# Loads, stores and direct copies of a strided slice: turns by groups of eight batches, one batch per direct copy

## The chip, the cores and the metric

The kernel runs on one core of a Trainium2 chip. The time is device microseconds (us) of one execution; lower is better. Some executions come out slow: more than 1.5% above the fastest of the same kernel. They are left out, and kernels are compared by their fast executions alone, taken on the same chip in the same rounds. A run here is one kernel tried on the chip.

## The reference

```python
# x: float32 [32, 1024, 512]; start, stop, stride = 0, 512, 2
def reference(x, start, stop, stride):
    return x[:, start:stop:stride, :].astype(np.float32)      # [32, 256, 512]
```

Nothing is computed. Every second row of the first 512 rows of each batch is copied: 32 batches of 256 rows of 2 KB, 16.78 MB read and 16.78 MB written.

## The kernel before

Each batch is split by the parity of its output row. One half goes from DRAM to DRAM (a "direct copy", on the gpsimd queue). The other half goes through SBUF: a load and later a store. `apart(b)` says which half is which. A direct copy and a load each serve two batches (512 KB); a store serves one (256 KB).

```python
def apart(b):
    return 1 - (b >> 1 & 1)

def two(t, b, step, parity):       # rows of one parity, of the batches b and b + step
    return t[b : b + step + 1 : step].rearrange("b (p two) d -> two p b d", two=2)[parity]
...
for g in range(0, B, EIGHT):
    for i, (b, step) in enumerate(((0, 5), (2, 5), (1, 3), (3, 3))):
        b += g
        at = g + 2 * i
        (sp, act)[i % 2].dma_start(held[at // 2], two(src, at, 1, 1 - apart(at)))        # load
        pool.dma_start(two(out, b, step, apart(b)), two(src, b, step, apart(b)))         # direct
for b in range(B):
    to = out[b].rearrange("(p two) d -> two p d", two=2)[1 - apart(b)]
    sp.dma_start(to, held[b // 2][:, b % 2])                                             # store
```

All loads come before all stores in program order. The framework adds the waits: eight DMAs may be under way on the gpsimd queue, and eight on the sync and scalar queues together.

## Time and profile before

| what | value | how to read it |
|---|---|---|
| time | 79.45 us, median of 3 (79.29 to 79.64) | |
| span of the profiled execution | 77.4 us | first instruction to last |
| first and last data packet | 1.8 and 76.1 us | all DMA work lies between them |
| data packets' time / 16 engines | 73.0 us | 74.3 us lie between first and last packet, so engines are nearly never idle |
| direct copies ended | 55.6 us | of the gpsimd queue's packets |
| loads ended | 48.8 us | of the scalar queue's packets |

A 2 KB packet takes 84 ns in the median and a 4 KB packet of the gpsimd queue 159 ns. Throughout, **late** is a packet over 40 ns above that. **Excess** is all time above it, summed over packets; 16 us of excess cost 1 us of time, as there are 16 engines. **Idle** is the time from first to last data packet less all data packets' time / 16. The small packets that report a DMA's completion count as idle (0.6 us before), and packets that overlap make it smaller, so it is a net figure.

### The profile page before, as it was taken

To read this page: it belongs to the slowest core of one execution; us is meant where nothing else is said; L and a number is where in the kernel's file an instruction comes from. 1 tells how busy PE (TensorE), PEld (TensorE's weight loads), DVE (VectorE), ACT (ScalarE), POOL (GpSimd) and SP (SyncE) were. 2 spreads that over 40 slices of the span, in tenths; PEclk is the share of its full clock that TensorE was granted. 3 is DMA by queue.
4 is the path that set the end of the run, shared out by engine and by line. 5 is a ranking of instruction groups with operands and counts; after the bars stand their busy time and mean duration, and the time that the engine had idled before them with its cause. 6 is when DMAs were issued, how large, how long until landed. Compare 5 with 4: busy or idle time off the path is not lost. (4 is left out here: it accounts for less than half of the span.)

```text
span 77.4 us, 113 instructions
## 1 busy us (share of the span) xinstructions
POOL 11.3 (15%) x20
## 2 busy tenths in 40 slices
POOL 4995003303023031130000000000000000000000
DMA  0799999999999999999999999999999999999960
GB/s 7 235 303 334 332 281 347 327 310 386 351 349 363 364 314 358 358 321 333 323 300 310 347 307 357 413 392 339 402 404 405 375 356 347 361 356 353 350 216 20
DMA packets 11264, 25.17 MB, mean 325 GB/s; under 512 B 1024, under 2 KB 1024, under 8 KB 11264
## 3 DMA queue, kind: packets, MB, share of 16 engines
q1 hardware_dynamic: 6784, 12.59, 48.1%
q0 software_dynamic: 2304, 8.39, 29.3%
q10 hardware_dynamic: 2176, 4.19, 17.7%
HBM read 16.78 MB, written 16.78 MB: 434 GB/s over the span
## 5 line engine op out<-in xcount | busy, mean ns | idle before, releaser
L37 POOL DMA_DIRECT2D out_dram<-in_x_dram x16 | 11.1, 696 | 22.6 <-DMA out_dram<-in_x_dram 21.8
L57 POOL MEMSET const-float32-0.0<- 128x1 f32 x1 | 0.1, 99 | 0.2 <-issue 0.2
L57 POOL MEMSET const-bfloat16-1.0<- 128x1 bf16 x1 | 0.1, 102 | 0.0
L57 POOL MEMSET const-uint8-127<- 128x1 uint8 x1 | 0.1, 100 | 0.0
L57 POOL MEMSET const-float32-1.0<- 128x1 f32 x1 | 0.1, 99 | 0.0
## 6 DMA issues: line engine op xcount, KB each, us to landing
out_dram<-in_x_dram POOLq DMA_DIRECT2D x16, 512.0 KB, 23.6
out_dram<-held SPq DMA_DIRECT2D x32, 256.0 KB, 6.1
held<-in_x_dram ACTq DMA_DIRECT2D x8, 512.0 KB, 22.9
held<-in_x_dram SPq DMA_DIRECT2D x8, 512.0 KB, 22.7
```

Source lines behind the costliest of these rows:

```text
L37: pool.dma_start(two(out, b, step, apart(b)), two(src, b, step, apart(b)))
L57: nc = _bacc.Bacc("TRN2", target_bir_lowering=False, num_devices=1)
```

## The change

Its intent: reading and writing shall be mixed all along, instead of reading first and writing last. Loads run one group of eight batches ahead; then the group's stores follow on the same two queues. Direct copies are issued one batch at a time.

```diff
-    sp, act, pool = nc.sync, nc.scalar, nc.gpsimd
+    queues = (nc.sync, nc.scalar)
+    groups = range(0, B, EIGHT)
+
+    def one(t, b, parity):
+        return t[b].rearrange("(p two) d -> two p d", two=2)[parity]
+
     with tc.tile_pool(name="io", bufs=1) as io:
         held = [io.tile([P, 2, D], x.dtype, name=f"held{i}") for i in range(B // 2)]
-        for g in range(0, B, EIGHT):
-            for i, (b, step) in enumerate(((0, 5), (2, 5), (1, 3), (3, 3))):
-                b += g
-                at = g + 2 * i
-                (sp, act)[i % 2].dma_start(held[at // 2], two(src, at, 1, 1 - apart(at)))
-                pool.dma_start(two(out, b, step, apart(b)), two(src, b, step, apart(b)))
+
+        def load(g):
+            for b in range(g, g + EIGHT, 2):
+                queues[b // 2 % 2].dma_start(held[b // 2], two(src, b, 1, 1 - apart(b)))
+
+        def store(g):
+            for b in range(g, g + EIGHT):
+                queues[b % 2].dma_start(one(out, b, 1 - apart(b)), held[b // 2][:, b % 2])
+
         for b in range(B):
-            to = out[b].rearrange("(p two) d -> two p d", two=2)[1 - apart(b)]
-            sp.dma_start(to, held[b // 2][:, b % 2])
+            nc.gpsimd.dma_start(one(out, b, apart(b)), one(src, b, apart(b)))
+        load(0)
+        for g in groups:
+            if g + EIGHT < B:
+                load(g + EIGHT)
+            store(g)
```

Three things change: the turns, the second queue with stores, and one batch per direct copy.

## The prediction

> **What bounds the kernel now.** I read the page first for who works at all, then the queues, then stretches of the span, then the single packets.
>
> ```profile
> span 77.4 us, 113 instructions
> ...
> DMA  0799999999999999999999999999999999999960
> GB/s 7 235 303 334 332 281 347 327 310 386 351 349 363 364 314 358 358 321 333 323 300 310 347 307 357 413 392 339 402 404 405 375 356 347 361 356 353 350 216 20
> ...
> q1 hardware_dynamic: 6784, 12.59, 48.1%
> q0 software_dynamic: 2304, 8.39, 29.3%
> q10 hardware_dynamic: 2176, 4.19, 17.7%
> ```
>
> No compute engine matters. The 16 DMA engines are 90% busy or more in every slice but the first two and the last two, while the rate wanders between 281 and 413 GB/s. So nothing starves: the time is the sum of all packets' times over 16 engines. From the kernel, q0 is the gpsimd queue (direct copies), q10 the scalar queue (half of the loads), q1 the sync queue (the other half and all stores). The shares add to 95.1%, or 73.6 us of 77.4; the rest is the 1.8 us before the first data packet and the 1.3 us after the last (at 76.1).
>
> The chain of waits ends in direct copies, POOL line 37, only because it was followed along one queue; the issues show that the queues are deep:
>
> ```profile
> POOL out_dram L37 <- DMA out_dram<-in_x_dram: 21.8, 8, 4.8
> ...
> out_dram<-in_x_dram POOLq DMA_DIRECT2D x16, 512.0 KB, 23.6
> out_dram<-held SPq DMA_DIRECT2D x32, 256.0 KB, 6.1
> ```
>
> Eight direct copies waited, the last eight of 16: eight may be under way at once. The sync and scalar queues have eight places together (the fifth load of each waits for the first of its queue, and each store for the DMA eight before it). A direct copy lands 23.6 us after issue, so POOL's waits cost nothing.
>
> Stretches, chosen where the packets of a queue begin or end (us from the start; POOL, clock, DMA share, GB/s):
>
> ```profile
> 2.00:6.00 4.00, 4.00 (x7) 1.00 0.89 274
> 6.00:48.00 42.00, 6.36 (x10) 1.00 1.00 334
> 48.00:54.00 6.00, 0.00 (x0) 1.00 1.02 384
> 54.00:60.00 6.00, 0.00 (x0) 1.00 1.04 403
> 60.00:75.00 15.00, 0.00 (x0) 1.00 1.02 345
> ```
>
> 2 to 6 is loads alone, 6 to 48 loads and direct copies, 48 to 54 direct copies and stores, then stores alone. (The first store is issued at 30.9 but sits behind the loads of its queue.) The rate is 334 while loads run and 384 to 403 when they have ended: this is what the change aims at. Is the loss caused by running loads together, or does each load bring it along? For that I counted the packet records of the trace (duration and size of every packet). A 2 KB packet has a median of 84 ns, a 4 KB packet of q0 159 ns. "Late" is over 40 ns more; excess is what the packets took over 84 or 159 ns:
> - Loads, 6 to 48: 3567 packets, 334 late (9.4%), by 229 ns on average; excess 77.9 us. Loads alone, 2 to 6: 536, 51 late (9.5%); excess 11.6 us.
> - Direct copies beside loads, 6 to 48: 1646 packets, 137 late (8.3%), by 206 ns; excess 29.4 us. Beside stores, 48 to 54: 366, 25 late (6.8%), by 229 ns; excess 5.9 us.
> - Stores, 48 to 60: 1481 packets, none late, excess 0. After 60: 2575, mean 95 ns, excess 28.9 us, as a broad stretch (5% over about 124 ns) and not as single late packets.
>
> So a packet that reads DRAM is late in 7 to 9.5% of cases whatever stands beside it, and one that only writes is not. This is the core of my prediction: the cost goes with the packet, not with the order.
>
> **What the Trainium skill says.** "DMA: Bandwidth & Descriptors", section "Issuing engines are not separate DMA queues": all queues run on the same 16 engines, and several issuers save only sequencer time. The trace agrees: the share is already 1.00 with three queues and 1.04 with one. The same page, "Queues, rings and completion order": an engine takes turns between queues packet by packet. It agrees: from 6 to 48 q0 with 4 KB packets moved 6.74 MB, the two 2 KB queues 7.31 MB. The same page, "Where 436 GB/s comes from": a ceiling of 435 GB/s; the best stretch here is 403, and 2 KB in 84 ns on 16 engines is 390. "HBM Reference", section "Latency": an access takes 0.2 us on average and more under load; late packets are late by 206 to 229 ns, but no run yet shows why.
>
> **The change, part by part.**
> 1. Bytes, row size (2 KB) and the halves of the rows stay. Direct copies become 32 of 256 KB in place of 16 of 512 KB: 16 more DMAs, so 256 more completion packets of 9 ns, 2.3 us / 16 = 0.14 us. POOL needs 0.69 us an issue now; even at that, 32 take 22 us, beside 50 us of transfer. Eight in flight are now 2.1 MB, at half of 340 GB/s some 12 us of work: still deep. Cost 0.1 us.
> 2. Floor, unchanged: 8192 packets x 84 ns + 2048 x 159 ns = 1013.8 us.
> 3. Read excess, by the above unchanged: 11.6 + 77.9 + 29.4 + 5.9 = 124.8 us. Floor and read excess / 16 = 71.2 us.
> 4. Stores alone after 60 us cost 28.9 / 16 = 1.8 us extra. That is what mixing can win, since beside direct copies stores have none. How much is left? In round robin q0 gets half of the bytes, so direct copies again end near 54 us (8.39 MB at 175 GB/s is 48 us, from 6 on). By then the other two queues have moved some 9.5 MB: loads of two groups, stores of one, loads of the third and part of a store group. About 7.3 MB follow, of which the last two store groups, 4.2 MB, are stores alone: 2048 packets against some 3700 now. The stretched mode began about 6 us (1100 packets) into stores alone; so 900 packets x 11 ns / 16 = 0.6 us remain, and 1.2 us are won.
> 5. Waits. DMAs strictly alternate between sync and scalar, so the one eight before is on the same queue: four places each, 1 to 2 MB. Each store's load was issued at least 8 DMAs before it. A store group of four x 256 KB per queue is some 5 us of work against a landing spread of about 2 us: no gap, or a few tenths at turns. I allow 0.3 us.
>
> Sum: 71.2 + 0.6 (stretched stores) + 1.3 (ramp and completion packets: today's 74.3 us between first and last packet less 1167.5 / 16 = 73.0) + 0.1 + 0.3 = 73.5 us, plus 3.1 us at the ends = a span of 76.6. Time over span is 79.45 - 77.40 = 2.05 in medians, 79.17 - 77.40 = 1.8 in the profiled run. That gives 78.5; I take 78.3, since the 6.8% beside stores is a little under 9%.
>
> **The rivals.**
> - Reading is what is overcrowded. From 6 to 48 all that moves is being read (334 GB/s), from 48 to 54 only two thirds. If late reads come from crowding, a mix at 380 all along gives 25.17 MB / 380 = 66 us, and a time near 71 to 72. For it: the rise to 384 at 48 us, and 6.8 against 8.3%. Against it: 25 and 137 cases do not separate these, loads without direct copies are late as often, and the mean rises merely because stores replace loads.
> - Reads and writes disturb each other, or one batch per direct copy meets worse addresses (now each 4 KB packet pairs rows of two batches, then two rows of one). Late reads at 11% in place of 9 would add 125 x 2/9 / 16 = 1.7 us: 80 to 81. Stores beside direct copies show no disturbance, but loads beside stores stand nowhere in this trace.
> - Four places per queue run dry at each turn. Five turns at 0.7 us would bring 81 to 82. The landing spread of some 2 us against 5 us of work speaks against it.
> - The stretched stores come back whole, as they need only stores from two queues: 79.5.
>
> **Range and chances.** The middle, 78.3, stands 0.4 us over the 2% line (77.9), and gain rests on a mode I can't explain; crowding would be a far larger gain. So 75.6 to 80.8, with 0.36 for faster, 0.50 within, 0.14 slower.
>
> **What would show it.** Right: DMA share stays at 1.00, late reads at 8 to 9.5% in every stretch, excess of reads near 125 us in sum, stores at 84 ns beside direct copies, direct copies ended near 54 us, last stores somewhat stretched. Wrong: late reads clearly under 7% where stores run beside loads (crowding; far faster), over 10% (disturbance; slower), slices with a share under 0.95 at the turns (places run dry), or direct copies that end last.

## The result, and the profile after

The changed kernel takes 83.73 us (median of 4, 83.38 to 83.89), against 79.37 us for the kernel before in the same rounds. The ratio is 1.0547 (95% interval 1.0491 to 1.0604). Ratios throughout are the mean time of one kernel's fast runs over that of the other's in the same rounds, so not quite the ratio of the medians quoted. The prediction, 78.3 with a range up to 80.8, was wrong, and on the wrong side.

The page of the changed kernel, with the span, the rows by 40 slices of 2.05 us, and the queues (packets, MB, share):

```profile
span 82.1 us, 145 instructions
...
DMA  0999989999999999999999999999999999799920
GB/s 16 264 309 340 273 221 373 367 280 338 330 372 417 376 318 318 337 236 302 285 349 316 299 374 400 381 321 328 326 250 297 300 332 361 293 391 394 375 85 8
...
q1 hardware_dynamic: 4480, 8.39, 31.3%
q10 hardware_dynamic: 4480, 8.39, 31.0%
q0 software_dynamic: 2560, 8.39, 30.7%
```

The engines are nearly as busy as before, save for an 8 early on and a 7 near the end. The GB/s row has lost its shape: instead of a flat start and a fast later part it swings from 417 down to 236. The bytes are the same. Each byte of the gpsimd queue, q0, now takes longer: 30.7% of 82.1 us against 29.3% of 77.4.

Stretches of the changed kernel (from:to, length, POOL busy and count, clock, DMA share, GB/s):

```profile
22.00:28.00 6.00, 1.79 (x4) 1.00 1.03 385
34.00:38.00 4.00, 1.57 (x3) 1.00 1.00 267
48.00:52.00 4.00, 1.05 (x2) 1.00 1.04 395
58.00:64.00 6.00, 0.00 (x0) 1.00 0.99 283
70.00:74.00 4.00, 0.00 (x0) 1.00 0.92 349
```

```profile
28.00:34.00 6.00, 1.57 (x3) 1.00 1.06 333
52.00:58.00 6.00, 0.00 (x0) 1.00 1.06 337
69.00:71.00 2.00, 0.00 (x0) 1.00 0.73 280
```

By counting the packets of each queue in order one sees what stood at its head. From 23 and from 47 us on, both queues start a group of stores: 385 and 395 GB/s. From 34 and from 58 us on they turn from stores back to loads: 267 and 283 GB/s, with engines that are counted as busy. The stores before such a turn suffer first: loads are issued again at 28.8 and 53.0 us, and until the loads' own packets come, 20% of the stores are late (28 to 34 and 52 to 58 us), against 0.3% in the 3 us before. From 69 to 71 us the share is 0.73: neither queue issued a store between 67.0 and 70.3 us, so some engines had no work left while others lagged.

The same count shows that the mix came out otherwise than intended. Both queues turn at nearly the same time, so only 507 of the 4096 load packets start in a half microsecond in which a store starts too. What runs beside loads, or beside stores, all along is the direct copies.

The packet records split the loss. From first to last data packet it is 78.9 us against 74.3, so 4.7 us more by the unrounded times:

| | before | changed | difference / 16 engines |
|---|---|---|---|
| direct copies: late, excess | 7.9%, 35.4 us | 14.6%, 72.3 us | +2.3 us |
| loads: late, excess | 9.4%, 89.6 us | 9.0%, 86.6 us | -0.2 us |
| stores: late, excess | 2.6%, 28.9 us | 5.8%, 36.8 us | +0.5 us |
| idle engines | 1.3 us | 3.4 us | +2.1 us |

### The profile page after: what moved, and what is told of

It is laid out like the page before. It is cut to its first block, busy times and chain, and to the rows that moved or that the text cites. A ratio compares the mean times of both kernels' runs of the same rounds, so it can differ in the third digit from the quotient of the medians.

```text
span 82.1 us, 145 instructions
## 1 busy us (share of the span) xinstructions
POOL 17.0 (21%) x36
## 3 DMA queue, kind: packets, MB, share of 16 engines
q0 software_dynamic: 2560, 8.39, 30.7%
HBM read 16.78 MB, written 16.78 MB: 409 GB/s over the span
## 4 chain that ended last, share of the span: by engine, by line
DMA 54%; POOL 5%; issue 3%; POOLq 1%; PEldq 0%
DMA out_dram<-in_x_dram 54%; POOL out_dram L46 5%; POOLq L82 1%; PEldq L82 0%
## 5 line engine op out<-in xcount | busy, mean ns | idle before, releaser
L46 POOL DMA_DIRECT2D out_dram<-in_x_dram x32 | 16.8, 527 | 34.2 <-DMA out_dram<-in_x_dram 33.4
```

What stands on the lines that cost most here:

```text
L46: nc.gpsimd.dma_start(one(out, b, apart(b)), one(src, b, apart(b)))
```

## The experiments

The kernel before runs at 79.2 to 79.4 us in all rounds below. The runs without direct copies, and the one with direct copies only, were executed twice, all others four or five times. The diffs are cuts: lines that only follow from the ones shown are left out.

### One part of the change at a time

**Only one batch per direct copy** (kernel before otherwise):

```diff
-                pool.dma_start(two(out, b, step, apart(b)), two(src, b, step, apart(b)))
+                for c in (at, at + 1):
+                    pool.dma_start(one(out, c, apart(c)), one(src, c, apart(c)))
```

> The kernel before with only its direct copies changed: 32 of one batch each in place of 16 of two. Theory P (one batch per direct copy makes the copies late twice as often, because each 4 KB packet then holds two neighbouring rows of one batch): excess of the direct copies rises from 35 to about 72 us, +2.3 us of time, 81.7. Theory M (stores and loads running beside each other and beside the direct copies make them late): excess stays near 35 us and the time at 79.4 to 79.6. Theory Q (two queues with stores, four places each, let DMA engines run dry): 79.4 to 79.6.

Measured: 81.52 us, ratio 1.0286 (1.0238 to 1.0335). The excess of the direct copies is 71.9 us, as theory P said. But the excess of loads and stores together fell from 118.6 to 89 us, so packets' time rose by 0.4 us only, and idle rose by 2.3 us, from 1.3 to 3.6. The loss is in idle engines, which theory P had not named. The end shows it. The same two stretches of the kernel before, then of this one:

```profile
70.00:74.00 4.00, 0.00 (x0) 1.00 1.04 347
74.00:77.00 3.00, 0.00 (x0) 1.00 0.28 103
```

```profile
70.00:74.00 4.00, 0.00 (x0) 1.00 1.05 360
74.00:77.00 3.00, 0.00 (x0) 1.00 0.67 225
```

Before, the engines are nearly done at 75 us. Here the share is two thirds until 77 us. From 76.5 to 78.8 us only 6 or 7 packets of 84 ns start in each half microsecond, which is the work of one engine: fifteen have run dry and one still drags. The semaphore updates tell how far: a DMA counts complete in 16 steps, read here as one for each engine, and the time from the first to the last step is the landing spread. For direct copies it is 0.9 to 1.7 us all along in the kernel before. Here it climbs from 0.9 to 7.1 us. Late in that climb several engines are behind; in the stores from 65 to 74 us it is one, 3.1 to 3.4 us after the first, while the other fifteen are done within 0.9 us. In the last store these are done within 0.6 us, and the one comes 2.9 us after the first.

**The changed kernel with the direct copies of before:**

```diff
-        for b in range(B):
-            nc.gpsimd.dma_start(one(out, b, apart(b)), one(src, b, apart(b)))
+        for g in groups:
+            for b, step in ((0, 5), (2, 5), (1, 3), (3, 3)):
+                b += g
+                nc.gpsimd.dma_start(two(out, b, step, apart(b)), two(src, b, step, apart(b)))
```

> The changed kernel with the direct copies of before: 16 of two batches each, everything else as changed. Theory P: excess of the direct copies back near 35 us, time about 81.4 (the 2.1 us of idle engines stay). Theories M and Q: excess of direct copies stays near 72 us, time 83.4 to 83.8.

Measured: 82.75 us, ratio 1.042 (1.0371 to 1.0468). It lies between what P and what M and Q said: pairs win back only 1.3 points of the 5.5. Its profiled execution was a slow one, so its packets are not used.

**Only the second queue with stores** (kernel before otherwise):

```diff
-            sp.dma_start(to, held[b // 2][:, b % 2])
+            (sp, act)[b % 2].dma_start(to, held[b // 2][:, b % 2])
```

> The kernel before with its stores dealt to the sync and scalar queues by turns instead of all to sync; still all loads first, pairs in the direct copies. Theory Q: engines idle or waiting near the end rise by about 2 us as in the changed kernel, 81 to 81.5. Theory M and P: no change of the mix in the first 48 us, so 79 to 79.6; it could even gain, since stores begin on both queues at once and the slow stores-alone stretch is spread.

Measured: 79.52 us, ratio 1.0018 (0.9977 to 1.006), idle 1.5 us. Theory Q falls for a second queue by itself.

**Only the turns** (changed kernel, with direct copies in pairs and all stores on sync):

```diff
-                queues[b % 2].dma_start(one(out, b, 1 - apart(b)), held[b // 2][:, b % 2])
+                nc.sync.dma_start(one(out, b, 1 - apart(b)), held[b // 2][:, b % 2])
```

> The turns alone: loads and stores by turns of eight batches in program order, but all stores on the sync queue as before, and direct copies in pairs as before. Theory M: direct copies late twice as often, 81.5 to 83.7. Theory Q: no idle engines, 79.4 to 80. Theory P: 79.4 to 80.

Measured: 81.74 us, ratio 1.0321 (1.0284 to 1.0359). Direct copies are late in 12.0% of cases with 63.9 us of excess, the other queues have 142 us. All excess together is 206 us against 154 before, +3.3 us; idle is 0.5 us against 1.3. So the turns cost packet time, while one batch per copy costs idle time. The time is in M's range, though direct copies are late half again as often and not twice; P's and Q's forecasts fail. The changed kernel with the direct copies of before differs from this one by the second queue with stores alone: 1.042 against 1.0321 in the same rounds, so with turns that queue costs about 1%. Factors of 1.029, 1.002 and 1.032 would make 1.064; together they make 1.055, so they don't simply add up.

Its trace has a stretch without any direct copy:

```profile
56.00:59.50 3.50, 0.00 (x0) 1.00 1.05 404
60.00:63.00 3.00, 0.00 (x0) 1.00 1.16 177
64.00:68.00 4.00, 0.00 (x0) 1.00 1.05 371
```

Until 59.5 us stores run alone at 404 GB/s, none late. At 58.3 and 59.0 us the sync queue issues the next two loads. From 60 to 63 us packets that are, by their order on the queue, still the last stores crawl at 177 GB/s: 84% of them late, by 143 ns. The share of 1.16 says that every engine is occupied, and that packets even overlap.

### Turns without direct copies

These kernels leave half of the output unwritten, to see loads and stores alone. First the kernel before without its direct copies:

```diff
-                pool.dma_start(two(out, b, step, apart(b)), two(src, b, step, apart(b)))
```

> The kernel before without its direct copies: half of the output stays unwritten, wrong on purpose. Only a base for the next run. Loads 8.39 MB at the 311 GB/s seen at the start, 27 us, stores 8.39 MB at 370, 23 us, ends 5 us: about 55 us.

Measured: 55.26 us (ratio to the kernel before 0.6966). Loads are late in 7.1 to 7.7% of cases, and all excess is 110 us.

Then the changed kernel without its direct copies:

```diff
-        for b in range(B):
-            nc.gpsimd.dma_start(one(out, b, apart(b)), one(src, b, apart(b)))
```

> The changed kernel without its direct copies, wrong on purpose in the same way. Theory T (a turn from stores to loads on a queue is itself slow: 170 to 250 GB/s for 2 to 4 us, as at 34 to 36 and 58 to 64 us of the changed kernel's trace): slow stretches at both such turns although no direct copy runs, and 3 to 6 us more than the run without direct copies in the order of before. Theory M (loads and stores beside the direct copies make those late): no more than 1 us of difference.

Measured: 58.67 us (0.7396), 3.4 us more; excess 166 us, so (166 - 110) / 16 = 3.5 us, the whole difference. Stretches of this run, and of the one in the order of before:

```profile
15.00:19.00 4.00, 0.00 (x0) 1.00 1.05 404
19.50:22.50 3.00, 0.00 (x0) 1.00 1.08 180
23.00:29.00 6.00, 0.00 (x0) 1.00 1.01 288
30.00:33.00 3.00, 0.00 (x0) 1.00 1.06 408
33.50:35.00 1.50, 0.00 (x0) 1.00 1.08 190
```

```profile
4.00:27.00 23.00, 0.00 (x0) 1.00 1.01 322
29.00:33.00 4.00, 0.00 (x0) 1.00 1.06 406
```

Stores alone run at 404 to 408 in both. With turns, each time loads are about to follow stores there are some 2 to 3 us at 180 to 190 GB/s, and the loads after them go at 288 where loads alone did 322. Direct copies are not needed for it, so theory M as I had put it falls, and T stood for the moment. By packets, the stores' crawl costs 53 us of excess and the loads 29 us more than in the order of before; 27 us less of it falls on the other stores. The loads were not late because stores ran beside them: from 24 to 28.5 us none did, and 12.1% were late.

**Six turns instead of two** (`EIGHT = 4` in place of 8):

> No direct copies (wrong on purpose), turns by groups of four batches instead of eight, so each queue turns from stores to loads six times instead of two. Theory T (each such turn costs a fixed time; 58.7 - 55.3 = 3.4 us for two turns, 1.7 us each): 55.3 + 6 x 1.7 = 65.5 us, at least 62. Rival (the loss of the run with turns of eight comes from how much of the loads overlaps with stores at all, not from the number of turns): 58 to 60.

Measured: 60.71 us (0.7642). That is 5.5 us over the order of before, not 10. A fixed price of 1.7 us per turn is refuted; the rival's 58 to 60 us is missed too, if narrowly.

**No queue turns at all**: loads all on scalar, stores all on sync:

```diff
-                queues[b // 2 % 2].dma_start(held[b // 2], two(src, b, 1, 1 - apart(b)))
+                nc.scalar.dma_start(held[b // 2], two(src, b, 1, 1 - apart(b)))
-                queues[b % 2].dma_start(one(out, b, 1 - apart(b)), held[b // 2][:, b % 2])
+                nc.sync.dma_start(one(out, b, 1 - apart(b)), held[b // 2][:, b % 2])
```

> No direct copies (wrong on purpose), turns of eight in program order, but all loads on the scalar queue and all stores on the sync queue, so no queue ever turns. Theory T (the turn within one queue is what costs): 54 to 56 us, no stretch under 250 GB/s after the start. Rival R (loads that begin while stores are under way slow down in DRAM or in the engines whatever their queue): 58 us or more, slow stretches.

Measured: 57.81 us (0.7278), 2.6 us over the order of before, and a little under the 58 us that R had asked for. Its stretches decide:

```profile
11.00:13.00 2.00, 0.00 (x0) 1.00 1.05 403
13.50:15.00 1.50, 0.00 (x0) 1.00 1.13 178
16.00:50.00 34.00, 0.00 (x0) 1.00 1.01 324
```

The crawl at 178 GB/s is there, in stores of a queue that holds nothing but stores, when loads are about to come again on the other queue. So a turn within one queue isn't needed, and theory T falls. Of theory R one half stays: loads that begin while stores run without loads slow the stores. That reads and writes slow each other whenever they run side by side is not shown. Loads here are late in 12.0% of cases against 7.1 to 7.7% in the order of before, but it is 12.4% up to 9 us, when hardly a store had begun, and 13.0% beside stores from 20 to 50 us; from 10.5 to 13 us, beside stores, not one is late. That all loads stand on one queue here is a further difference, which no run tries alone.

**Loads that wait for the stores before them** (one set of four buffers, reused in reverse order; `load(g)` directly before `store(g)`):

```diff
-        held = [io.tile([P, 2, D], x.dtype, name=f"held{i}") for i in range(B // 2)]
+        held = [io.tile([P, 2, D], x.dtype, name=f"held{i}") for i in range(EIGHT // 2)]
-            for b in range(g, g + EIGHT):
+            for b in reversed(range(g, g + EIGHT)):
```

> No direct copies (wrong on purpose), turns of eight batches as changed, but with one set of four buffers for all groups, filled again in the reverse order of the stores, so that loads of a group can start only when the stores before have (nearly all) landed. Theory R (reads that start or run beside unfinished writes slow both): stores at 84 ns to their end, under 3% of them late apart from the last group, loads late at the 7 to 8% of the run without turns; the time is long through empty queues, 62 to 72 us, but the packets' excess is at most that of the run in the order of before (110 us). Theory T (the turn itself costs): stores of 200 ns before each group of loads all the same, excess over 150 us.

Measured: 60.83 us (0.7678), excess 172 us, slow stretches as before. This looks like T, but the kernel failed as a test. The trace shows the first load of the second group issued at 11.4 us, while the last store of the first group landed at 17.6 us: the buffers had come free in another order than I had meant, so reads and unfinished writes did overlap. It decides nothing between T and R.

### Why one batch per direct copy costs

**One batch, rows far apart in a packet** (kernel before otherwise):

```diff
+def far(t, b, parity):
+    return t[b].rearrange("(h p two) d -> two p h d", two=2, h=2)[parity]
-                pool.dma_start(two(out, b, step, apart(b)), two(src, b, step, apart(b)))
+                for c in (at, at + 1):
+                    pool.dma_start(far(out, c, apart(c)), far(src, c, apart(c)))
```

> The kernel before with 32 direct copies of one batch each, but their rows dealt so that the two rows of a 4 KB packet lie half a batch apart instead of next to each other. Theory N (neighbouring rows in a packet make some DMA engines fall behind): landing spread back from 7 to 1 to 2 us, excess of the direct copies near 36 us, time 79.2 to 79.8. Theory S (the number of direct copies, 32 small ones with half the bytes under way, is what costs): as the run with one batch each in plain order, 81.2 to 81.8, landing spread 5 to 7 us.

Measured: 81.13 us, ratio 1.0222 (1.018 to 1.0265); landing spread of the direct copies up to 6.1 us. Theory N falls. (Which two rows share a packet is read from the order of the access pattern; the records don't show it.)

**32 copies, but each of half of the rows of two batches:**

```diff
-                pool.dma_start(two(out, b, step, apart(b)), two(src, b, step, apart(b)))
+                to, of = two(out, b, step, apart(b)), two(src, b, step, apart(b))
+                for h in (0, P // 2):
+                    pool.dma_start(to[h : h + P // 2], of[h : h + P // 2])
```

> The kernel before with its 16 direct copies each cut in two: 32 copies of 256 KB, each of half of the rows of the same two batches. Theory S (number and size of the direct copies, or half the bytes under way, let DMA engines drift apart): 81.0 to 81.8, landing spread 4 to 7 us. Theory B (what matters is that a copy reads and writes in two batches at once): 79.2 to 79.8, landing spread 1 to 2.5 us.

Measured: 79.37 us, ratio 1.0 (0.9964 to 1.0036); landing spread of the direct copies 1.2 to 2.4 us. The number and size of the copies, and the bytes under way, are the same as with one batch each, and the loss is gone. Theory S falls.

**Two neighbouring batches** instead of batches five or three apart:

```diff
-                pool.dma_start(two(out, b, step, apart(b)), two(src, b, step, apart(b)))
+                pool.dma_start(two(out, at, 1, apart(at)), two(src, at, 1, apart(at)))
```

> The kernel before with direct copies of two neighbouring batches (0 and 1, 2 and 3) instead of batches five or three apart. Theory S: as before, 79.2 to 79.8. Theory B in its strict form (the distance of the two batches matters too): 80.5 to 82.

Measured: 79.37 us, ratio 0.9977 (0.9938 to 1.0016). The distance of the two batches doesn't matter. So copies over two batches keep the engines together, and copies within one don't. Whether it is the second batch that does it or the distance within a copy is not separated: the two rows of a packet lie half a batch (0.5 MB of x) apart in the run with far rows, and at least one batch (2 MB) in all copies over two. Why an engine falls behind its neighbours, no run here shows either: the records do not name the engine of a packet.

### Attempts to beat both kernels

**Everything copied directly**, in pairs, without loads and stores:

```diff
-                (sp, act)[i % 2].dma_start(held[at // 2], two(src, at, 1, 1 - apart(at)))
-                pool.dma_start(two(out, b, step, apart(b)), two(src, b, step, apart(b)))
+                for parity in (apart(b), 1 - apart(b)):
+                    pool.dma_start(two(out, b, step, parity), two(src, b, step, parity))
```

> A candidate to beat both: no loads and stores, all 16.78 MB by 32 direct copies of two batches on the gpsimd queue. If a 4 KB packet keeps to 176 ns: 4096 x 176 / 16 = 45 us, about 52 us in all. If DRAM limits (before reached at most 634 GB/s of reads and writes together, from 48 to 54 us): 33.6 MB / 634 = 53 us, 60 us in all. If copies alone get in each other's way, packets of over 250 ns and 75 us or more.

Measured: 84.44 us, ratio 1.0644. The queue line of its page:

```profile
q0 software_dynamic: 4608, 16.78, 90.1%
```

A third fewer bytes pass the engines, and it is still slower. A 4 KB packet takes 289 ns in the mean instead of 176, 37% are late, by 350 ns. In 77.4 us from first to last packet 16.78 MB move, 217 GB/s.

**Direct copies held back until the loads have landed**, by a small copy on gpsimd that reads the last two loaded tiles (before the direct copies in program order):

```diff
+        for n in (B // 2 - 2, B // 2 - 1):
+            pool.tensor_copy(late, held[n][:, 1, D - 1 :])
```

> The kernel before with its direct copies held back until all loads have landed: loads alone, then stores beside direct copies. If loads suffer from writes beside them and direct copies hardly from stores (6.8% late from 48 to 54 us of before): loads 27 us as without direct copies, then 16.8 MB at 384 GB/s, 44 us, ends 5 us: 76 to 77. If direct copies suffer wherever they run beside stores (late over 12%, as in the kernels that take turns): 79 or more.

Measured: 81.79 us, ratio 1.031 (1.0263 to 1.0358). The kernel was not what I meant: in the trace ten direct copies had been moved ahead of the wait and ran beside the loads, and six came after it. What came of the six is telling all the same:

```profile
44.50:46.00 1.50, 1.45 (x4) 1.00 1.06 407
46.00:51.00 5.00, 2.98 (x5) 1.00 1.07 215
```

At 44.7 us the first held-back copy is issued; no load follows any more. Stores alone had been running at 407 GB/s, and then all crawls at 215, with 64% of the stores late from 46 to 51 us. So it is not loads as such: reading that resumes beside writes does it, by direct copies too. From 50 us on 18.2% of the direct packets are late, beside stores alone. They do not come evenly: from 52 to 54 us not one was over 165 ns. So the same mix runs clean at one time and badly at another.

**More direct copies, fewer loads and stores**: 5 or 3 of the 16 pairs of loads are given up.

```diff
+def goes_direct(n):
+    return n % 3 == 2          # and: n % 5 == 4
-                (sp, act)[i % 2].dma_start(held[at // 2], two(src, at, 1, 1 - apart(at)))
+                if goes_direct(at // 2):
+                    pool.dma_start(two(out, at, 1, 1 - apart(at)), two(src, at, 1, 1 - apart(at)))
+                else:
+                    (sp, act)[i % 2].dma_start(held[at // 2], two(src, at, 1, 1 - apart(at)))
```

> The kernel before with 5 of the 16 pairs of loads and their stores given up, these halves copied directly too: 11.0 MB direct, 5.8 MB loaded and stored. Theory A (the sum of packet times is the bound; 2 KB cost 102 + 84 ns by way of SBUF and 88 ns directly): 2816 x 105 + 2816 x 86 + 2688 x 177 ns = 1014 us / 16 = 63.4, ends 5: about 69 to 71. Theory C (reads and writes together are limited, as in the run that copies everything directly, and then packets just take longer): 78 to 82.

> The same with 3 of the 16 pairs given up: 10.0 MB direct, 6.8 MB loaded and stored. Theory A: 3328 x 105 + 3328 x 86 + 2432 x 177 ns = 1066 us / 16 = 66.6, ends 5: 72 to 74. Theory C: 78 to 80.

Measured: 81.45 us (ratio 1.0271, 1.0236 to 1.0307) for five, 80.58 us (1.0145, 1.0094 to 1.0197) for three. Theory A, the sum of fixed packet times, falls by over 10 us for the first. Two stretches of it, beside loads and then beside stores:

```profile
20.00:30.00 10.00, 2.29 (x4) 1.00 0.99 332
40.00:70.00 30.00, 3.44 (x5) 1.00 1.02 282
```

Beside stores alone (42 to 70 us) 36.4% of 1265 direct packets are late, by 268 ns; beside loads it is 4.9% in the stretch shown and 10.3% from 6 to 30 us.

**Loads on the gpsimd queue**, with its 4 KB packets: the scalar queue's half, or all.

```diff
-                (sp, act)[i % 2].dma_start(held[at // 2], two(src, at, 1, 1 - apart(at)))
+                (sp, pool)[i % 2].dma_start(held[at // 2], two(src, at, 1, 1 - apart(at)))   # or pool for all
```

> The kernel before with the scalar queue's half of the loads moved to the gpsimd queue, where packets are 4 KB. If the sum of packet times is the bound: 2048 packets of 107 ns become 1024 of about 177: (219 - 181) / 16 = 2.4 us less, 77. If lateness goes with bytes and not with packets, or mixing on one queue disturbs: 79 to 80.

> The kernel before with all loads on the gpsimd queue among the direct copies, and only stores on the sync queue. Sum of packet times alone: 4.8 us less, 74.5. But stores now start early and run beside loads from 10 us on, so theory R says late reads at 12% or more, 77 to 82.

Measured: 79.76 us (1.0068, 1.0022 to 1.0113) for half, 82.87 us (1.0419, 1.0342 to 1.0496) for all. In the first, the gpsimd queue's packets are late in 9.5% of cases beside loads (up to 33 us) and in 23.0% beside stores (40 to 60 us); the stores themselves there are never late. What the larger packets won is given back. The second, in which stores are issued beside reads nearly all along, loses more; its profiled execution was a slow one, so only its times are used.

No run beat the kernel before. More direct copies (three pairs) and half of the loads on gpsimd are within 2% of it.

## Why the prediction was wrong

**The step that failed** is the one it called its core: "the cost goes with the packet, not with the order". With the prediction's own terms, between first and last packet (73.5 us predicted, 78.9 measured):

| term | predicted | measured | difference / 16 engines |
|---|---|---|---|
| excess of loads | 89.5 us | 86.6 us | -0.2 us |
| excess of direct copies | 35.3 us | 72.3 us | +2.3 us |
| excess of stores | 10 us (0.6 us x 16) | 36.8 us | +1.7 us |
| ramp, completion packets and waits (idle) | 1.7 us | 3.4 us | +1.7 us |

For loads the core held. For direct copies it rested on 366 packets from 48 to 54 us, 25 of them late (6.8%), taken as what happens beside stores. That stretch was not typical. Beside stores alone, direct packets were late in 36.4% of cases with five pairs given up, in 18.2% with copies held back, and gpsimd packets in 23.0% with half of the loads there. In the order of before they ran beside stores for only about 7 us, and then were through. In the changed kernel itself the neighbour doesn't settle it: beside loads alone, 10.8% of direct packets are late from 6 to 22 us and 20.7% from 36 to 46 us. And "one that only writes is not [late]" failed for stores when loads were issued behind them (20% late). In the kernel with the turns alone, all excess is 206 us in place of 154: 3.3 us. (A slip of reading that changes nothing: the 3567 "loads" from 6 to 48 us include 39 stores.)

**Crowding of reads**, the rival that kept the middle low, fell: loads were late as often as before (9.0 against 9.4%), direct copies more often. **Disturbance**, the second rival, was right in kind; its 80 to 81 was too low for the whole change. It put one batch per copy and the mix into one figure of 1.7 us. Alone they cost 2.9% and 3.2%, some 2.3 and 2.5 us.

**Part 1**, direct copies of one batch "cost 0.1 us". The count of packets and POOL's time were right: POOL is busy for 16.8 us with them, under the 22 allowed. What failed is that only number, depth and issue time were asked for. The copies' cost was in engines that drift apart: a landing spread of 7 us instead of 1.7, and 2.3 us of idle.

**Part 4**, 1.2 us to win from the stretched stores: in the changed kernel, stores from 70 to 76 us did run with 1 us of excess in all, so there the mode is nearly gone. That much was won, but the stores before the turns lost more, and their excess rose in sum (36.8 against 28.9 us). Direct copies were to end near 54 us; they ended at 63.3.

**Part 5**, waits at the turns, 0.3 us: right that the two queues with four places each don't matter by themselves (ratio 1.0018); with turns they cost about 1%. And it took a landing spread of 2 us as given. With a spread of 6 to 7 us against 5 us of work, four places do run dry, as from 69 to 71 us, and idle rose by 2.1 us in the whole change. How that splits between the parts in the combined kernel is not separated; with the turns alone, idle is lower than before.

What would have warned me: loads that come back while stores run stood nowhere in the trace. I wrote so of loads beside stores, and still carried rates over.

What stays open: by which mechanism reads that resume beside writes slow them (that stores crawl for 2 to 5 us at 177 to 215 GB/s is shown, with loads and with direct copies, on one queue and on two), why loads after a turn stay later even alone, why a mix of direct copies and stores is now clean and now has a third of its reads late, and why copies within one batch let engines drift.

## What to carry to other kernels

On a DMA-bound kernel, treat the rate of a mix of reads and writes as unknown until a stretch of the trace has that same mix for long enough; here no interleaving tried was faster than reading first and writing last. When the DMA engines are all busy, look also at how far the 16 of them drift apart in the landings of one DMA: a copy's shape can cost idle time that no packet shows. Change one thing at a time: alone, two of the three parts cost some 3% each and the third nothing; with turns that third cost about 1%.

## What the Trainium skill lacked or had wrong

- "DMA: Bandwidth & Descriptors" is right that several issuers bring no bandwidth ("Issuing engines are not separate DMA queues"; a second queue with stores gave a ratio of 1.0018). No page says that the order of reads and writes on those engines costs time: turns alone, 1.0321; stores that fall from 404 to 177 GB/s as reads come back.
- No page has a rate that it says is for DRAM to DRAM copies by themselves. The nearest, in "DMA: Bandwidth & Descriptors", section "Latency and other measured facts", is for copies between HBM tensors on the sync and scalar queues: 207 GB/s per direction at a row pitch of 512 KiB, 214 with a padded pitch; it doesn't say whether they pass through SBUF. Here direct copies alone move 217 GB/s (37% of 4 KB packets late), while stores alone reach 404 to 408 and loads of 2 KB rows alone 322.
- The same section says that DMA engines 7 and 15 are usually slower than the others, without a figure. No page says that the shape of a copy decides how far engines drift apart. Here copies within one batch reach a spread of 6 to 7 us and cost 2.2 to 2.9%; copies over two batches, with loads and stores as before, show 0.9 to 2.7 us of spread and cost nothing. In the run with one batch per copy a single engine ends 3 us behind; the records don't say which.
